# One decoder layer on one core: w_out gated earlier, four schedules around the MLP rewritten

## The chip, the cores and the metric

The kernel runs on one core of a Trainium2 chip. The metric is the device time of one execution in microseconds (us). TensorE (PE) does matmuls into PSUM, VectorE (DVE) and ScalarE (ACT) do the elementwise work, GpSimd (POOL) a little of it, and nearly all DMAs are issued from the queue of SyncE (SP). Each engine takes its instructions in a fixed order; an instruction that waits holds up all behind it on its engine.

## The reference

One layer (DEPTH 1) on x of 1024 tokens by 1024 features, fp32. Cut to what matters here:

```python
merged = sigmoid(ga) * (ya @ w_a) + sigmoid(gm) * (ym @ w_m)
x = x + gt_a * (merged @ w_out)                      # gt_a: one gate per output feature
h = rms_norm(x, norm_ffn_g) * (1 + sc_f) + sh_f
x = x + gt_f * (square(relu(h @ w_ff1)) @ w_ff2)     # 4096 hidden features
```

`ya` comes from an 8-head differential attention, `ym` from an mLSTM; both are computed before the part that changes, save the last attention head.

## The kernel before, in words

Every fp32 operand of a matmul is split into a high part (a rounded copy, written by ACT) and a low part (the difference, written by DVE; `parts`, lines 317 to 320), and a product is three matmuls. One call of `mm_block` is 12 matmuls of 128x512.

The large products are done by Strassen-Winograd: 7 block products in place of 8, numbered 1 to 7, with sums of blocks of the left operand, sums of blocks of the right operand, and sums of the outputs. These sums are DVE work. The stages, in order of time:

- **Last attention head beside w_m.** `at_core` (line 1202) for head 7 is woven with `m_unit` (line 1324): 32 half-steps of 12 matmuls for `ym @ w_m`, each output multiplied by its gate (`gated`, line 1312) and stored to `mb_d` from POOL's queue. 24 of the 32 are woven with the head, 8 come after it.
- **w_a, then w_out**, as two jobs of `Chunks` (line 1535). A chunk is 7 products of 48 matmuls (4 output rows of blocks, 12 each). `prep` makes the operands of a product one product ahead of `run`. `pieces` (line 1655) loads w_out in 8 pieces of 512 KB during the w_a job, and `behind` (line 1694) multiplies each piece by half the gate `gta` on DVE. `out_o` adds the residual rows `xr`, squares and sums them (`square`, `rms`), stores x to `xn_d` and scales the rows.
- **w_ff1** in 16 groups of 256 hidden features (`Ff1`, line 1820). `norm_feat` (line 1804) transposes the normalised rows and applies scale and shift, half on ACT and half on DVE. Groups 0 and 1 start while the right operands of products 7, 5, 6, 3 and 4 are still being made; each later group runs its 7 products of 12 matmuls. `out` applies relu and square; the blocks a11, a12, a21, a22 of the activation and their sums (7: a11-a21, 5: a21+a22, 6: that minus a11, 3: a12 minus that) are made on DVE and stored to `act_d[1..7]`, the left operands of the next stage.
- **w_ff2** as four chunks (lines 1998 to 2052). Chunk c needs the groups 4c to 4c+3. `fetch_act` loads a left operand (2 x 512 KB), `fetch_ff2` loads a block of w_ff2 and multiplies it by half the other gate on DVE. `out_f` adds each product to the accumulators `au, aa, av, ab, ac`, four of which are first loaded whole, 1 MB each, with the residual from `xn_d`.

The order of the instructions on each engine is not the program's: a planner simulates the program with its own costs, and issues whatever is ready and has a free buffer, earlier program text first. Buffers are drawn by tag (`BUFS`, line 57): "u" and "b" have 2 of 4 KB each, "e" and "v" 4, "r" 8, "f" 5 of 2 KB, "x" 4 large ones, "wh"/"wl" 2 each for split weights. A later tile of a tag waits until an earlier one has had its last reader. PSUM has three tags of 2, 3 and 3 banks; `Chunks.run` takes its four banks from one set or the other in turn (`self.sets`).

## Time and profile before

| what | value |
|---|---|
| median of 3 runs (lowest to highest) | 2050.91 us (2049.52 to 2053.59) |
| profiled execution: time, span | 2053.98 us, 2052.2 us |
| mean granted TensorE clock | 0.983 |
| PE busy | 1981.0 us, 97% |
| DVE busy | 1644.7 us, 80% |
| ACT busy | 1046.2 us, 51% |
| DMA | 296.71 MB, mean 145 GB/s |

The time is that of the profiled execution; the span runs from the first to the last instruction of its trace. Busy times overlap, and are averages over stages that have different limits: how near an engine is to its limit has to be read stage by stage. The granted clock is the share of full TensorE speed that the throttle allowed; where it is under 1, the same matmuls take longer while PE counts as busy.

### The profile page before, as it was taken

To read this page: it belongs to the slowest core of one execution; us is meant where nothing else is said; L and a number is where in the kernel's file an instruction comes from. 1 tells how busy PE (TensorE), PEld (TensorE's weight loads), DVE (VectorE), ACT (ScalarE), POOL (GpSimd) and SP (SyncE) were. 2 spreads that over 40 slices of the span, in tenths; PEclk is the share of its full clock that TensorE was granted. 3 is DMA by queue.
4 is the path that set the end of the run, shared out by engine and by line. 5 is a ranking of instruction groups with operands and counts; after the bars stand their busy time and mean duration, and the time that the engine had idled before them with its cause. 6 is when DMAs were issued, how large, how long until landed. Compare 5 with 4: busy or idle time off the path is not lost.

```text
span 2052.2 us, 30148 instructions
## 1 busy us (share of the span) xinstructions
PE 1981.0 (97%) x11193; PEld 1716.0 (84%) x11193; DVE 1644.7 (80%) x2892; ACT 1046.2 (51%) x1966; POOL 56.4 (3%) x150
## 2 busy tenths in 40 slices
PE   5999999999999999999999999999899999999999
PEld 5999988888888899999998788777688887788887
DVE  7977668987766568999979667999867767998896
ACT  5523324544656557777757535446544544433332
POOL 0000000000111000000000110000000000000000
PEclk7999999999999999999999999999999999999999
DMA  8376633336555342222223474513444447744531
GB/s 289 105 218 213 190 116 110 110 108 201 176 154 175 112 111 63 83 63 83 68 78 118 158 248 159 169 42 134 164 148 156 146 147 247 276 148 150 164 111 74
DMA packets 201834, 296.71 MB, mean 145 GB/s; under 512 B 13956, under 2 KB 114975, under 8 KB 201687
## 3 DMA queue, kind: packets, MB, share of 16 engines
q1 hardware_dynamic: 198806, 285.35, 43.4%
q0 software_dynamic: 2880, 9.44, 1.2%
q8 instruction: 88, 1.44, 0.3%
q14 instruction: 60, 0.48, 0.1%
HBM read 206.43 MB, written 79.93 MB: 140 GB/s over the span
## 4 chain that ended last, share of the span: by engine, by line
PE 74%; DVE 10%; DMA 7%; issue 4%; ACT 3%; POOL 1%; SPq 0%; POOLq 0%; DVEq 0%; ACTq 0%
PE cps L328 16%; PE pc L328 9%; PE pb L328 9%; PE pa L328 9%; PE pd L328 5%; PE ps L166 4%; PE ps L165 4%; PE ps L167 4%; PE lg L1219 3%; PE pv L1272 3%; DMA ex<-ea_d 2%; PE tp L1252 1%; PE ops L585 1%; DVE s_op L138 1%; DVE t_op L138 1%
## 5 line engine op out<-in xcount | busy, mean ns | idle before, releaser
L328 PE MATMUL cps<-t_op,s_op 128*128 128x512 f32 x2016 | 471.7, 395 | 11.7 <-ACT s_op L320 5.9
L328 PEld LDWEIGHTS cps<-t_op,s_op 128*128 128x128 f32 x2016 | 379.4, 189 | 101.2 <-ACT s_op L320 7.4
L320 ACT ACTIVATE w_op<-w_st 128x512 fp32r<-128x512 f32 (+1 forms) x197 | 135.8, 704 | 199.4 <-PE pb L328 61.7
L138 DVE TENSOR_TENSOR w_op<-w_st,w_op 128x512 fp32r<-128x512 f32 (+1 forms) x197 | 150.4, 782 | 25.1 <-ACT w_op L320 23.1
L165 PE MATMUL ps<-w_hi,hT 128*128 128x256 f32 x512 | 146.5, 286 | 0.0
L166 PE MATMUL ps<-w_lo,hT 128*128 128x256 f32 x512 | 145.9, 285 | 0.0
L167 PE MATMUL ps<-w_hi,hT 128*128 128x256 f32 x512 | 145.6, 284 | 0.0
L320 ACT ACTIVATE s_op<-act 128x1024 fp32r<-128x1024 f32 x56 | 58.5, 1051 | 144.7 <-PE cps L328 108.4
L1229 ACT ACTIVATE ee<-ee,mneg 128x256 f32<-128x256 f32 (+7 forms) x128 | 98.3, 769 | 10.0 <-DVE mneg L1225 9.7
L328 PE MATMUL pc<-bt,w_op 128*128 128x512 f32 x384 | 97.0, 399 | 6.1 <-ACT w_op L320 5.1
L1219 PE MATMUL lg<-kb,qe 128*128 128x512 f32 (+3 forms) x384 | 96.8, 360 | 5.0 <-DVE mneg L1225 4.4
L166 PEld LDWEIGHTS ps<-w_lo,hT 128*128 128x128 f32 x512 | 97.6, 191 | 1.4 <-issue 0.9
L165 PEld LDWEIGHTS ps<-w_hi,hT 128*128 128x128 f32 x512 | 97.5, 190 | 0.5
L167 PEld LDWEIGHTS ps<-w_hi,hT 128*128 128x128 f32 x512 | 97.6, 191 | 0.3
L328 PE MATMUL pa<-b,w_op 128*128 128x512 f32 x384 | 94.9, 397 | 0.4 <-DVE w_op L138 0.4
L328 PEld LDWEIGHTS pc<-bt,w_op 128*128 128x128 f32 x384 | 71.8, 190 | 26.5 <-ACT w_op L320 5.9
L316 DVE TENSOR_TENSOR acc<-cps,acc 128x512 f32<-128x512 f32 x116 | 77.0, 684 | 13.1 <-PE cps L328 12.8
L328 PEld LDWEIGHTS pa<-b,w_op 128*128 128x128 f32 x384 | 73.2, 192 | 15.9 <-DVE w_op L138 0.8
L1225 DVE CUSTOM_DVE_ANT_0 ee<-lg,bs 128x512 f32<-128x512 f32 (+4 forms) x128 | 69.9, 559 | 8.8 <-PE lg L1219 7.8
L138 DVE TENSOR_TENSOR s_op<-act,s_op 128x1024 fp32r<-128x1024 f32 x56 | 68.2, 1220 | 6.9 <-ACT s_op L320 6.9
L1219 PEld LDWEIGHTS lg<-kb,qe 128*128 128x128 f32 x384 | 61.2, 192 | 13.1 <-DVE mneg L1225 8.2
L328 PE MATMUL pa<-hT,w_op 128*128 128x512 f32 x264 | 64.1, 392 | 0.0
(404 smaller groups left out, 4747.8 us busy)
## 6 DMA issues: line engine op xcount, KB each, us to landing
w_st<-in_w_in_dram SPq DMA_DIRECT2D x72, 512.0 KB, 4.0
act<-act_d SPq DMA_DIRECT2D x56, 512.0 KB, 3.6
w_st<-in_w_ff_dram SPq DMA_DIRECT2D x36, 512.0 KB, 4.8
crow<-in_w_ada_dram SPq DMA_DIRECT2D x32, 512.0 KB, 4.3
w<-in_w_ff_dram SPq DMA_DIRECT2D x32, 512.0 KB, 4.8
act_d<-s SPq DMA_DIRECT2D x48, 256.0 KB, 2.0
wa<-in_w_ada_dram SPq DMA_DIRECT2D x16, 512.0 KB, 4.7
mq_d<-cv SPq DMA_DIRECT2D x16, 512.0 KB, 2.6
```

The source lines that it names most:

```text
L138: return (nc.gpsimd if pool else nc.vector).tensor_tensor(dst, src, hi.bitcast(F32), op=ALU.subtract)
L165: nc.tensor.matmul(o, lhsT=ah, rhs=bh, start=first, stop=False)
L166: nc.tensor.matmul(o, lhsT=ah, rhs=bl, start=False, stop=False)
L167: nc.tensor.matmul(o, lhsT=al, rhs=bh, start=False, stop=last)
L316: (nc.gpsimd if pick(pool, n) else nc.vector).tensor_tensor(o, a, b, op=ALU.add)
L320: nc.scalar.activation(dst[0], src, AF.Copy)
L328: nc.tensor.matmul(ps, lhsT=p, rhs=q, start=first and k == 0 and r == 0, stop=k == 3 and r == 2, skip_group_check=True,)
L585: nc.tensor.matmul(o, lhsT=a[ra], rhs=w[rb][:, k, :], start=k == 0 and ra == rb and j % 2 == 0, stop=k == KT - 1 and ra == 1, skip_group_c ...
L1219: nc.tensor.matmul(lg[:, 0:max(256, w)], lhsT=hd["q"][hf][e][:, r, q4 * P:(q4 + 1) * P], rhs=hd["k"][e][:, c0:c0 + max(256, w)], start=r = ...
L1225: nc.vector.tensor_tensor_reduce(ee[:, c0:c0 + w], lg[:, 0:w], hd["bs"][:, n - c0 - w:n - c0][:, ::-1], -0.125, first, ALU.add, ALU.min, last,
L1229: nc.scalar.activation(ee[:, 0:n], ee[:, 0:n], AF.Exp, bias=mneg[:, e:e + 1], scale=-1.0, accum_out=ssum[:, e:e + 1])
L1272: nc.tensor.matmul(pv[:, 0:256], lhsT=pts[kk // 4][r][:, (kk % 4) * P:(kk % 4 + 1) * P], rhs=v, start=kk == 0 and r == 0, stop=kk == qi an ...
```

## The change

It has five parts.

1. **w_out.** In the last attention head's stage, half the gate is made (`gta`), and 8 row blocks of w_out (128x1024, 512 KB) are loaded into "u" tiles, multiplied by it on DVE and stored to a new DRAM tensor `wo_d`, each load placed in the text with half-step 12, 14, ... 26 of `m_unit` and each multiplication and store three half-steps later. `pieces` then loads from `wo_d`, and `behind` is gone.
2. **First groups of w_ff1.** Groups 0 and 1 store their four blocks only; their four sums are made during groups 6 and 8 from blocks loaded back (`late_sums`). For groups 0 to 3 the square of the first block moves from DVE to ACT, and the second half of `norm_feat` is all on ACT.
3. **Last group of w_ff1.** A class of its own, with the product order 1, 6, 5, 3, 7, 4, 2; its four sums are made after the ninth product of w_ff2.
4. **First chunk of w_ff2.** Order 1, 2, 7, 4, 5, 6, 3, the bank sets begin with the other set, and the first values of `aa` and `av` are copied by ACT, as that of `au` was.
5. **Residual.** `ac` and `ab` are loaded whole after products 0 and 2; the residual of `aa` and `av` comes in 8 loads of 128x512, each added on DVE, around products 7 to 15.

```diff
--- before.py
+++ after.py
@@ -76,6 +76,7 @@
     xn_d = dp.tile([S, D], F32, name="xn_d")
     gt_d = dp.tile([2, P, D], F32, name="gt_d")
     ub_d = dp.tile([AH, S + P], F32, name="ub_d")
+    wo_d = dp.tile([D, D], F32, name="wo_d")
     ea_d = dp.tile([32, S], F32, name="ea_d")
 
 
@@ -1525,6 +1526,24 @@
         else:
             ym = ActX("ym")
             units = sum((m_unit(ym, u) for u in range(4)), [])
+            gta = wt("b", [P, D], "gta")
+            nc.sync.dma_start(gta, gt_d[0])
+
+            nc.vector.tensor_scalar(gta, gta, 0.5, None, op0=ALU.mult)
+            wos = {}
+
+            def fetch_wo(r):
+                wos[r] = wt("u", [P, D], "wor")
+                nc.sync.dma_start(wos[r], w_out[0][r * P:(r + 1) * P, :])
+
+            def gate_wo(r):
+                w = wos.pop(r)
+                nc.vector.tensor_tensor(w, w, gta, op=ALU.mult)
+                nc.sync.dma_start(wo_d[r * P:(r + 1) * P, :], w)
+
+            for r in range(8):
+                units[12 + 2 * r] = lambda r=r, f=units[12 + 2 * r]: (fetch_wo(r), f())
+                units[15 + 2 * r] = lambda r=r, f=units[15 + 2 * r]: (gate_wo(r), f())
             filler += reload(ym, ym_d, False) + units[0:12 * 2]
         weave(core, filler)
         late = nlate
@@ -1686,15 +1705,6 @@
     (m11, m21), (m12, m22), (u1, u2) = ((t[:, 0], t[:, 1]) for t in mgs)
     load[:] = [0.0, 0.0]
     ch = Chunks(xp.tile([P, 2, 4, 512], F32R, name="s_op", tag="x"))
-    gta = wp.tile([P, D], F32, name="gta", tag="ws", bufs=2)
-    nc.sync.dma_start(gta, gt_d[0])
-
-    nc.vector.tensor_scalar(gta, gta, 0.5, None, op0=ALU.mult)
-
-    def behind(t, c):
-        g = gta[:, c * 512:c * 512 + 512]
-        nc.vector.tensor_tensor(t, t, g.unsqueeze(1).to_broadcast([P, 2, 512]), op=ALU.mult)
-
     def merge(dst, c, f0, t0):
 
         mb = wt("m", [P, 512], "mb")
@@ -1731,13 +1741,13 @@
     for n in range(7):
         ch.prep()
         if n == 4:
-            wo = pieces("e", "wo", w_out[0], False, (11,), behind)
+            wo = pieces("e", "wo", wo_d, False, (11,))
         ch.run()
         if n == 5:
 
-            pieces("v", "wo", w_out[0], False, (21,), behind, wo)
-            pieces("e", "wo", w_out[0], False, (12,), behind, wo)
-            pieces("v", "wo", w_out[0], False, (22,), behind, wo)
+            pieces("v", "wo", wo_d, False, (21,), into=wo)
+            pieces("e", "wo", wo_d, False, (12,), into=wo)
+            pieces("v", "wo", wo_d, False, (22,), into=wo)
             xr = fetch("r", "xr", x2, range(8))
             ssq = cp.tile([P, NT, 2], F32, name="ssq")
             ssf = cp.tile([P, NT], F32, name="ssf")
@@ -1801,6 +1811,8 @@
 
     act_d = {i: dp.tile([NG * P, 512], F32, name=f"act{i}_d") for i in range(1, 8)}
 
+    ORDER_L = (1, 6, 5, 3, 7, 4, 2)
+
     def norm_feat(js, act, dst):
 
 
@@ -1837,7 +1849,10 @@
             c = into
             if c is None:
                 c = wt("f", [P, 512], "c")
-            if b is None:
+            if b is None and self.g < 4:
+                nc.scalar.activation(c, a, AF.Relu)
+                nc.scalar.activation(c, c, AF.Square)
+            elif b is None:
                 nc.scalar.activation(c, a, AF.Relu)
                 nc.vector.tensor_tensor(c, a, c, op=ALU.mult)
             else:
@@ -1850,10 +1865,13 @@
             elif (t, hf) == (1, 1):
                 self.a22 = c
                 self.put(4, c)
-                if self.g < 4:
+                if 1 < self.g < 4:
 
                     self.a11 = wt("f", [P, 512], "a11")
                     nc.sync.dma_start(self.a11, act_d[1][self.g * P:(self.g + 1) * P, :])
+            elif self.g in LATE:
+
+                self.put(5 if (t, hf) == (0, 1) else 2, c)
             elif (t, hf) == (0, 1):
 
                 s3 = wt("f", [P, 512], "s3")
@@ -1869,6 +1887,103 @@
                 sub(self.s24[:, 1], c, self.s24[:, 0], False)
                 self.put(3, self.s24[:, 1])
 
+    class Ff1Last(Ff1):
+
+
+        def weights(self, order):
+            (a11, a21), (a12, a22) = self.st
+            for q, i in enumerate(order):
+                if q % 2 == 0:
+                    t2 = w_tile().rearrange("p (s r k c) -> p s r k c", s=2, r=2, k=4)
+                src = {1: a11, 2: a12, 4: a22, 5: a21, 6: a11, 7: a11, 3: None}[i]
+                if i == 6:
+                    add(a21, a21, a22, *self.pool)
+                    sub(a11, a21, a11, *self.pool)
+                elif i == 3:
+                    src = self.s3()
+                    sub(src, a12, a11, *self.pool)
+                elif i == 7:
+
+                    sub(a11, a22, a11, *self.pool)
+                self.operand(i, t2[:, q % 2], src)
+
+        def p6(self):
+            pd, m1 = bank("mm", "pd"), self.m1[0]
+            self.prod(6, 0, pd, True)
+            add(m1, pd, m1, False)
+
+        def p5(self):
+            self.pb[0] = bank("pa", "pb5")
+            self.m7[0] = wt("m", [P, 512], "m7")
+            self.prod(5, 0, self.pb[0], True)
+            nc.scalar.activation(self.m7[0], self.pb[0], AF.Copy)
+
+        def p7(self):
+            m7 = self.m7[0]
+            self.pc[0] = bank("pb", "pc")
+            self.prod(7, 0, self.pc[0], True)
+            add(m7, self.pc[0], m7, False)
+            self.out(1, 1, 0, m7, self.m1[0], m7)
+
+        def out(self, t, hf, n, a, b, into):
+            c = into
+            if c is None:
+                c = wt("f", [P, 512], "c")
+            if b is None:
+                nc.scalar.activation(c, a, AF.Relu)
+            else:
+                add(c, a, b, False)
+                nc.scalar.activation(c, c, AF.Relu)
+            nc.scalar.activation(c, c, AF.Square)
+            if (t, hf) == (0, 1):
+                self.a21 = c
+            elif (t, hf) == (1, 1):
+                self.a22 = c
+                self.put(4, c)
+            elif (t, hf) == (1, 0):
+                self.a12 = c
+                self.put(2, c)
+            else:
+                self.put(1, c)
+                self.a11 = c
+
+        def sums(self):
+            a11, a12, a21, a22 = self.a11, self.a12, self.a21, self.a22
+            s3 = wt("f", [P, 512], "s3")
+            sub(s3, a11, a21, False)
+            self.put(7, s3)
+            add(a21, a21, a22, False)
+            self.put(5, a21)
+            sub(a11, a21, a11, False)
+            self.put(6, a11)
+            sub(a12, a12, a11, False)
+            self.put(3, a12)
+
+    LATE = (0, 1)
+
+    def late_sums(g):
+
+        x, y = (wt("e", [P, 2, 512], "late") for _ in range(2))
+        a11, a21, a22, a12 = x[:, 0], x[:, 1], y[:, 0], y[:, 1]
+
+        def fetch():
+            for v, i in ((a11, 1), (a21, 5), (a22, 4), (a12, 2)):
+                nc.sync.dma_start(v, act_d[i][g.g * P:(g.g + 1) * P, :])
+
+        def one():
+            add(a22, a21, a22, False)
+            g.put(5, a22)
+            sub(a21, a11, a21, False)
+            g.put(7, a21)
+
+        def two():
+            sub(a11, a22, a11, False)
+            g.put(6, a11)
+            sub(a12, a12, a11, False)
+            g.put(3, a12)
+
+        return fetch, one, two
+
 
     eb = [wt("e", [P, 2, 512], f"eb{k}") for k in range(4)]
     e_at = lambda k: eb[k // 2][:, k % 2, :]
@@ -1882,7 +1997,7 @@
             B[i] = lambda k: (ts[k][:, 0, :], ts[k][:, 1, :])
 
     feat0 = norm_feat(range(4), (4, 5, 6, 7), e_at)
-    groups = [Ff1(g) for g in range(NG)]
+    groups = [Ff1(g) for g in range(NG - 1)] + [Ff1Last(NG - 1)]
     g0, g1, g2, g3 = groups[0:4]
 
     def half0(k):
@@ -1901,7 +2016,7 @@
     g1.load_first()
     rw = [wt("r", [P, 2, 512], "rw") for _ in range(4)]
     b_at = lambda k: rw[k // 2][:, k % 2, :]
-    feat1 = norm_feat(range(4, 8), (4, 5, 6, 7), b_at)
+    feat1 = norm_feat(range(4, 8), range(8), b_at)
 
     def right(i, k):
         b11, b21, b12, b22 = e_at(k), e_at(4 + k), b_at(k), b_at(4 + k)
@@ -1987,19 +2102,23 @@
         if g in (g2, g3):
             g.weights((7, 5, 6, 3, 4))
             run([g.p7, g.p5, g.p6, g.p3, g.p4])
+        elif g.g in (6, 8):
+            fetch, one, two = late_sums(groups[LATE[g.g // 2 - 3]])
+            g.weights((1, 7, 2, 5, 6, 3, 4))
+            run([fetch, g.p1, g.p7, g.p2, g.p5, one, g.p6, two, g.p3, g.p4])
         elif g is not groups[-1]:
             g.weights((1, 7, 2, 5, 6, 3, 4))
             run([g.p1, g.p7, g.p2, g.p5, g.p6, g.p3, g.p4])
         else:
-            g.weights((1, 7, 2, 5, 6, 3, 4))
-            run([g.p1, g.p7, g.p2, g.p5, g.p6, g.p3, g.p4])
+            g.weights(ORDER_L)
+            run([getattr(g, f"p{i}") for i in ORDER_L])
 
 
     def out_f(c, i, j, ps):
         d = {1: au, 7: av, 2: aa, 4: ac, 5: av, 6: au, 3: ab}[i]
         last = c == NC - 1
-        if i == 1 and c == 0:
-            nc.scalar.activation(au[:, j], ps, AF.Copy)
+        if c == 0 and i in (1, 2, 7):
+            nc.scalar.activation(d[:, j], ps, AF.Copy)
         elif i != 6 or not last:
             add(d[:, j], ps, d[:, j], False)
         if last:
@@ -2029,27 +2148,44 @@
         ms = {2: (11,), 3: (12,), 4: (22,), 5: (21,)}.get(n, ())
         fetch_ff2(c + 1, w2[c + 1], [(m, homes[c + 1][m]) for m in ms])
 
+    ORDER_F = [(1, 2, 7, 4, 5, 6, 3) if not c else ORDER_X for c in range(NC)]
     for c in range(NC):
         ch.add(
-            ORDER_X, None, w2[c], lambda i, j, ps, c=c: out_f(c, i, j, ps),
+            ORDER_F[c], None, w2[c], lambda i, j, ps, c=c: out_f(c, i, j, ps),
             lambda i, q, c=c: act.pop((c, i, q)),
         )
-    order = [(c, i) for c in range(NC) for i in ORDER_X]
+    order = [(c, i) for c in range(NC) for i in ORDER_F[c]]
+    ch.sets = 1
     fetch_act(0, 1)
     ch.prep()
+    fetch_ff2(0, w2[0], [(21, homes[0][21])])
+    fetch_act(0, 2)
     fetch_ff2(0, w2[0], [(12, homes[0][12]), (22, homes[0][22])])
     fetch_act(0, 7)
-    for q, t0, c0 in ((aa, 0, 0), (ab, 0, 512), (ac, 512, 0), (av, 512, 512)):
-        nc.sync.dma_start(q, xn_d[t0:t0 + 512, c0:c0 + 512].rearrange("(t p) c -> p t c", p=P))
-    fetch_ff2(0, w2[0], [(21, homes[0][21])])
-    fetch_act(0, 2)
     fetch_act(0, 4)
+
+    whole = {0: (ac, 512, 0), 2: (ab, 0, 512)}
+    joins = [(q, t0, c0, j) for q, t0, c0 in ((aa, 0, 0), (av, 4, 512)) for j in range(4)]
+    rows = {}
+
     for n in range(7 * NC):
         if n + 4 < len(order):
             fetch_act(*order[n + 4])
         ch.prep()
         chunk_part(n // 7, n % 7)
         ch.run()
+        if n == 8:
+            groups[-1].sums()
+        if n in whole:
+            q, t0, c0 = whole[n]
+            nc.sync.dma_start(q, xn_d[t0:t0 + 512, c0:c0 + 512].rearrange("(t p) c -> p t c", p=P))
+        if n - 1 in rows:
+            q, t0, c0, j = joins[n - 8]
+            add(q[:, j], q[:, j], rows.pop(n - 1), False)
+        if 7 <= n < 15:
+            q, t0, c0, j = joins[n - 7]
+            rows[n] = wt("m", [P, 512], "res")
+            nc.sync.dma_start(rows[n], xn_d[(t0 + j) * P:(t0 + j + 1) * P, c0:c0 + 512])
 
 
 # ---- launch: one core; inputs and outputs as the reference has them ----
```

## The prediction

> **What bounds the kernel now.** I read the page's busy times first, then the stretches of 50 us, then the waits of PE in the stretches where it idles.
>
> ```profile
> PE 1981.0 (97%) x11193; PEld 1716.0 (84%) x11193; DVE 1644.7 (80%) x2892; ACT 1046.2 (51%) x1966; POOL 56.4 (3%) x150
> ```
>
> The change adds and removes no matmul, so what it can win is idle time of PE (2052.2 - 1981.0 = 71 us of the span) and time at a lower granted clock. Here are the stretches it touches; columns are busy us of PE, PEld, DVE, ACT, POOL with instruction counts, then granted clock, DMA share, GB/s.
>
> ```profile
> 1100.00:1150.00 50.00, 42.67 (x223) 35.30 (x223) 45.15 (x118) 37.90 (x90) 2.66 (x4) 0.90 0.51 159
> 1150.00:1200.00 50.00, 49.88 (x250) 41.82 (x249) 29.03 (x49) 17.41 (x35) 4.39 (x8) 1.00 0.56 190
> 1300.00:1350.00 50.00, 45.20 (x186) 35.26 (x185) 50.00 (x67) 22.24 (x30) 0.00 (x0) 0.97 0.25 84
> 1400.00:1450.00 50.00, 46.20 (x205) 36.84 (x205) 46.22 (x78) 31.34 (x57) 1.77 (x2) 0.93 0.40 130
> 1450.00:1500.00 50.00, 43.93 (x182) 34.55 (x181) 38.07 (x62) 24.75 (x42) 0.00 (x0) 0.97 0.55 186
> 1550.00:1600.00 50.00, 50.00 (x218) 40.47 (x217) 34.89 (x56) 26.08 (x43) 0.00 (x0) 1.00 0.42 145
> 1700.00:1750.00 50.00, 45.76 (x191) 36.23 (x190) 37.56 (x50) 23.90 (x36) 0.00 (x0) 0.97 0.78 272
> 1750.00:1800.00 50.00, 47.63 (x207) 38.24 (x206) 46.80 (x49) 19.64 (x20) 0.00 (x0) 1.00 0.72 251
> 1815.00:1893.00 78.00, 78.00 (x341) 63.77 (x340) 71.32 (x80) 28.51 (x32) 0.00 (x0) 1.00 0.46 144
> ```
>
> PE is full wherever it is not starved. It is starved in four places, and the waits of PE there (us in total, times, longest) say by whom: 1300 to 1360 (w_out begins), 1360 to 1430 and 1430 to 1500 (w_ff1 begins), 1720 to 1800 (w_ff2 begins).
>
> ```profile
> PE cps L328 <- ACT t_op L320: 2.7, 1, 2.7
> PE cps L328 <- DVE t_op L138: 2.3, 3, 1.6
> ...
> PE tp L1810 <- DVE xr L1761: 2.0, 1, 2.0
> ...
> PE pc L328 <- ACT w_op L320: 5.1, 2, 3.7
> PE pd L328 <- ACT w_op L320: 1.0, 1, 1.0
> PE pc L328 <- DVE w_op L138: 1.0, 1, 1.0
> PE pd L328 <- DVE w_op L138: 0.4, 1, 0.4
> ...
> PE cps L328 <- ACT s_op L320: 5.9, 3, 3.2
> PE cps L328 <- DVE s_op L138: 0.7, 1, 0.7
> ```
>
> So 5.0, 2.0, 7.5 and 6.6 us. Each longer gap is followed by a stretch at a lower clock:
>
> ```profile
> 1340.00:1350.00 10.00, 6.78 (x22) 4.78 (x22) 10.00 (x15) 6.13 (x10) 0.00 (x0) 0.83 0.00 1
> 1400.00:1410.00 10.00, 7.65 (x27) 5.42 (x27) 9.02 (x17) 4.83 (x11) 1.77 (x2) 0.72 0.45 159
> 1460.00:1470.00 10.00, 6.30 (x21) 4.27 (x20) 9.78 (x17) 5.53 (x10) 0.00 (x0) 0.83 0.96 348
> 1740.00:1750.00 10.00, 6.81 (x24) 5.13 (x23) 8.95 (x12) 5.59 (x8) 0.00 (x0) 0.83 1.01 369
> ```
>
> A clock of 0.83 over 10 us costs 1.7 us, one of 0.72 costs 2.8. I charge 1.7 to each of the first, third and fourth place.
>
> **1. The gating leaves the w_out stage.** The tile view of `wo`: eight multiplications, and the DVE idle time before them, which waits on the loads.
>
> ```profile
> L1696 DVE TENSOR_TENSOR wo<-wo,gta x8: 1216/1224/1229, 1264.3 to 1310.1; 128x1024 f32<-128x1024 f32 x8
> ...
> DMA wo<-in_w_out_dram: 7.4, 4
> ...
> 1308.93 2.36 DVE L1696 TENSOR_TENSOR wo<-wo,gta 128x1024 f32<-128x1024 f32 x2
> ```
>
> DVE loses 8 x 1.22 = 9.8 us of work and up to 7.4 us of waiting, all ahead of 1311. From 1300 to 1350 it is busy for all 50 us, so a backlog is what starves PE, and 5.0 us of PE waiting need less relief than that. The last two multiplications, 2.36 us, stand directly before the operands of the first w_out product. Eight loads of the same size remain, now from `wo_d`. Value -(5.0 + 1.7) = -6.7; bounds -6.7 and 0 (the DVE finds other waits). I take -6.7, since 17.2 us of relief against 5.0 leaves a wide margin.
>
> **2. The gating arrives beside w_m.** Added on DVE: 8 x 1.22, and the scaling of `gta`, which it only moves by some tens of us: 9.8 us. Between 1150 and 1200 DVE is busy 29 of 50 us, so 21 us are free in that stretch alone while PE is full: nothing, as long as the stretch is PE's; without that cover 9.8 us. Added on SP: 8 loads, 8 stores and the earlier `gta` load, 8.5 MB in all. The stretch at risk is the one ahead of it, 1120 to 1150:
>
> ```profile
> 1120.00:1130.00 10.00, 6.58 (x30) 4.05 (x28) 9.74 (x36) 8.37 (x27) 0.54 (x1) 1.00 0.95 284
> ...
> 1121.31 6.40 SPq L1663 DMA_DIRECT2D wa<-in_w_a_dram  x4
> ...
> 1138.20 1.06 ACT L152 ACTIVATE w_hi<-w_st 128x1024 fp32r<-128x1024 f32 x1 [1.47 <-DMA w_st<-in_w_m_dram]
> ```
>
> The planner there puts four loads of w_a, wanted 100 us later, ahead of w_m's; ACT then waits for w_m with the softmax of the head behind it. The "u" and "b" buffers fall free at about that time, so the first two w_out loads and `gta` (1.5 MB) can go the same way: at 284 GB/s that is 5.5 us of DMA. Bounds 0 (they are issued after w_m's) and +5.5; no work leaves this stretch, which excludes a gain. I take +2, between the ends, because only a part of a shared delay falls on w_m's loads.
>
> **3. First groups of w_ff1.** Columns: min/median/max ns.
>
> ```profile
> L1815 DVE TENSOR_SCALAR rw<-tp,gsf,shf x4: 804/805/811, 1411.0 to 1424.2; 128x512 f32<-128x512 f32 x4
> ...
> L1842 DVE TENSOR_TENSOR c<-pa,c x16: 684/692/693, 1417.3 to 1720.2; 128x512 f32<-128x512 f32 x16
> ...
> L1813 ACT ACTIVATE rw<-tp,shf,gsf x4: 767/773/776, 1414.0 to 1425.1; 128x512 f32<-128x512 f32 x4
> ...
> 1463.46 0.68 DVE L313 TENSOR_TENSOR s<-c,a 128x512 f32<-128x512 f32 x1
> 1464.06 0.68 DVE L313 TENSOR_TENSOR s<-w_st 128x512 f32<-128x512 f32 x1
> ```
>
> DVE loses 8 sums (8 x 0.68), 4 squares (4 x 0.69) and 4 scalings (4 x 0.81): 11.4 us between 1411 and 1466. The sums stand right before the line `s<-w_st` at 1464.06, from which ACT makes the weight that ended PE's longest wait, 3.7 us. ACT gains 4 x 0.77 and 4 squarings of about the same length, some 6 us, in a stretch where it is busy 31 of 50 us. Of the 7.5 us of waits, 2.4 (the second `pc` wait of 5.1 - 3.7 = 1.4, and the 1.0 for DVE) come where group 3 starts behind group 2's sums, and these stay. So -(7.5 - 2.4 + 1.7) = -6.8; bounds -6.8 and 0 (ACT becomes what is late). I take -6, near the full end, as DVE had no idle time there. The moved sums go to groups 6 and 8 (1550 to 1650), where DVE has 15 of 50 us free: 8 x 0.68 and 8 loads of 256 KB, hidden by it; 5.4 us if not. The wait of 2.0 us at 1404 has its DVE chain before the scalings moved, so I leave it: 0, bounds -(2.0 + 2.8) and +2.
>
> **4. Start of w_ff2.** PE waits there for ACT, and ACT for a transfer:
>
> ```profile
> 1744.71 1.06 ACT L320 ACTIVATE s_op<-act 128x1024 fp32r<-128x1024 f32 x1 [1.17 <-DMA act<-act_d]
> ...
> L2043 SPq DMA_DIRECT2D acc<-xn_d x4: 386/481/590, 1715.8 to 1739.3; - x4
> ...
> DMA to landing us min/median/max: 10.0/10.0/10.0
> ```
>
> The DMA share is 1.01 from 1740 to 1750, and 4 MB of the queue are the residual: at that row's 369 GB/s they are 11 us, and the third product's wait is 5.9 + 0.7 in all. Afterwards the first three products need 2, 2 and 3 MB instead of 2, 3 and 2, with no residual ahead of them; at 369 GB/s a product of 11 us covers 4 MB. The four sums of the last group (4 x 0.68 on DVE) and their four stores go as well. -(6.6 + 1.7) = -8.3 at best, 0 if the new order of the last group frees its buffers too late. I take -6.5, as DVE, too, is nearly full there (46.8 of 50).
>
> **5. Chunks 0 and 1 of w_ff2.** Chunk 0 moves 8 adds to ACT copies; chunk 1 gets 8 residual adds and the 4 sums: 12 x 0.68 = 8.2 us. In 1815 to 1893, about one chunk, DVE is busy 71.3 of 78 us: 6.7 free, 1.5 short. Bounds 0 and +8.2 (cover gone); I take +1.5.
>
> **Sum.** -6.7 + 2 - 6 - 6.5 + 1.5 = -15.7 us. The profiled execution took 2053.98 us, 3 above the median of the runs; -15.7 on the median of 2050.91 is 2035.
>
> [...]
>
> **The rivals.**
> - *Slower: the round trip of w_out jams the queues beside w_m.* Only two "u" buffers serve eight load-multiply-store turns, so each load waits on SP until the store two turns before has landed, and the w_m, gate and w_a loads stand behind it. The tile that holds the split left operand of w_a's first products is drawn from the same "u" and "b" buffers, so w_a cannot prepare before the last turn is over. For it: the loads of w_a at 1121 show that the planner lets such work pass. Against: the stretch has 90 us and PE runs full in it. It decides when a turn's store (2.6 us for 512 KB, row below) is no longer covered by w_m work in hand: 8 x 2.6 = 20.8, and a clock loss of 1.7; -15.7 - 2 + 22.5 = +4.8, so 2056.
>
> ```profile
> mq_d<-cv SPq DMA_DIRECT2D x16, 512.0 KB, 2.6
> ```
>
>   [...]
> - *Half: the w_out stage stays as it is* because DVE's backlog there is made of splits and merges (1300 to 1350 has 65 other instructions), and w_ff2's start wins half: -15.7 + 6.7 + 3 = -6, so 2045. For it: DVE is full for 50 us. Against: the 17 us of relief.
> - *No change: the waits are renamed.* A planner that orders anew gives back elsewhere what it wins; 2051. For it: DVE is above 90% in most of the stages concerned.
>
> **How the numbers follow.** Likeliest 2035 with 0.64; half 0.14; no change 0.09; slower 0.13. The likeliest one's own range is 2026 to 2043: all terms at their good ends give -6.7 - 6.8 - 8.3 - 4.8 = -26.6, 2024, which is unlikely together. The range of 8 in 10 goes from 2024 to 2050. A measurement here can tell about 0.2%, 4.1 us: faster (under 2046.8) 0.64 + 0.11 = 0.75; same 0.03 + 0.09 = 0.12; slower 0.13.
>
> **What would show it.** Right: from w_out's first product on no PE wait over 1 us for `t_op`; no wait of 3 us on `w_op` as w_ff1 begins; no wait of ACT on `act` as w_ff2 begins, with the granted clock at 1.00 around it; PE still full in the chunk after the first. Step 2 is wrong if PE's idle time between 1120 and 1150 grows by over 5 us. The whole is wrong if the four places keep over half of their 21 us, or if PE starts w_a late.

## The result and the profile after

The changed kernel takes 2039.85 us (median of 6 runs, 2033.00 to 2041.01); the kernel before, run beside it, 2053.06 us (6 runs, 2049.52 to 2059.35). The ratio is 0.9927, 95% interval 0.9912 to 0.9943: faster, by 13.2 us in the medians. The profiled execution after is one of the short ones, 2033.65 us with a span of 2031.9; the profiled pair is 20.3 us apart, and 4.6 of that lies ahead of all that was changed.

To see this I cut both traces at five places. First the timeline of before, then that of after: the start of the last head (ACT), the first product of w_a (PE), the first transpose of w_ff1 (PE), the first product of w_ff2 (PE) and the last sum of the output (DVE). Columns: start us, us, engine, line, operation.

```profile
1096.67 1.04 ACT L1168 ACTIVATE sq<-raw 128x1024 f32<-128x1024 f32 x1
1233.86 26.44 PE L328 MATMUL cps<-t_op,s_op 128*128 128x512 f32 x114
1392.20 0.66 PE L1810 MATMUL tp<-ksq,xr 128*128 128x128 f32 x4 [0.32 <-DVE xr L316]
1730.21 2.10 PE L328 MATMUL cps<-t_op,s_op 128*128 128x512 f32 x8 [0.32 <-ACT s_op L320]
2048.45 0.69 DVE L316 TENSOR_TENSOR acc<-cps,acc 128x512 f32<-128x512 f32 x1 [2.03 <-PE cps L328]
```

```profile
1092.08 1.04 ACT L1169 ACTIVATE sq<-raw 128x1024 f32<-128x1024 f32 x1
1236.06 24.10 PE L329 MATMUL cps<-t_op,s_op 128*128 128x512 f32 x104
1388.50 0.66 PE L1822 MATMUL tp<-ksq,xr 128*128 128x128 f32 x4 [0.31 <-DVE xr L317]
1718.11 22.24 PE L329 MATMUL cps<-t_op,s_op 128*128 128x512 f32 x96
2028.01 0.69 DVE L317 TENSOR_TENSOR acc<-cps,acc 128x512 f32<-128x512 f32 x1 [2.03 <-PE cps L329]
```

The differences are four stages: **A** last head and w_m, **B** w_a and w_out, **C** w_ff1, **D** w_ff2. The same cuts were made in every kernel below (us):

| kernel | A | B | C | D |
|---|---|---|---|---|
| before | 137.2 | 158.3 | 338.0 | 318.2 |
| after | 144.0 | 152.4 | 329.6 | 309.9 |
| only_w_out | 142.4 | 154.7 | 340.0 | 317.0 |
| no_w_out | 134.3 | 158.8 | 328.6 | 309.7 |
| only_first | 135.4 | 158.6 | 329.4 | 317.9 |
| only_ff2 | 137.0 | 159.8 | 337.8 | 309.5 |
| dma_only | 143.4 | 152.5 | 328.8 | 310.6 |
| dve_only | 137.4 | 154.0 | 330.3 | 310.1 |
| pool_wm | 151.5 | 154.4 | 329.7 | 310.9 |
| no_w_out_pool | 137.6 | 161.3 | 329.9 | 309.7 |
| late_gates | 134.4 | 163.9 | 329.6 | 309.7 |
| sums_only | 143.6 | 155.7 | 334.3 | 310.7 |
| res_whole | 145.9 | 154.1 | 328.8 | 310.7 |
| last_plain | 143.4 | 155.4 | 331.2 | 312.4 |

What comes ahead of stage A is the same work in all of them, yet it took from 1091 to 1100 us. A stage is therefore a better measure of one part than a total is. Here are the stretches of after that answer to those shown of before; columns as there.

```profile
1150.00:1200.00 50.00, 44.86 (x227) 37.35 (x226) 30.68 (x50) 17.55 (x35) 3.83 (x7) 1.00 0.82 283
1200.00:1250.00 50.00, 47.17 (x216) 38.71 (x215) 31.71 (x41) 19.09 (x30) 5.40 (x9) 1.00 0.52 177
1300.00:1350.00 50.00, 48.23 (x208) 38.63 (x207) 48.94 (x66) 25.26 (x37) 0.00 (x0) 1.00 0.22 72
1400.00:1450.00 50.00, 49.34 (x226) 40.64 (x227) 46.15 (x78) 36.34 (x66) 1.07 (x1) 0.97 0.39 114
1450.00:1500.00 50.00, 47.63 (x201) 38.27 (x200) 33.07 (x53) 25.00 (x42) 0.00 (x0) 0.97 0.56 188
1700.00:1750.00 50.00, 50.00 (x219) 40.49 (x218) 44.50 (x49) 29.76 (x44) 0.00 (x0) 1.00 0.94 333
1750.00:1800.00 50.00, 50.00 (x219) 40.88 (x218) 46.07 (x52) 20.20 (x23) 0.00 (x0) 1.00 0.57 187
1800.00:1900.00 100.00, 100.00 (x437) 81.66 (x436) 93.88 (x110) 35.34 (x38) 0.00 (x0) 1.00 0.54 168
```

At w_out's start PE is busy 48.2 of 50 us, before 45.2. As w_ff1 begins it is 49.3 and 47.6, before 46.2 and 43.9. As w_ff2 begins it is full. The loss is in the first two rows: 44.9 and 47.2, where before had 49.9 and 50.0. The waits of PE in after, in two stretches (1100 to 1240, then 1245 to 1500), name what is left:

```profile
PE pv L1273 <- DVE ptl L1257: 4.0, 3, 3.1
...
PE tp L1290 <- DVE yt L1284: 2.2, 1, 2.2
PE ps L166 <- DVE sg L1320: 1.7, 1, 1.7
...
PE tp L1822 <- DVE xr L1771: 2.0, 1, 2.0
PE cps L329 <- DVE t_op L139: 1.8, 1, 1.8
PE pc L329 <- ACT w_op L321: 1.4, 1, 1.4
PE pc L329 <- DVE w_op L139: 1.0, 1, 1.0
```

The first three do not stand in before's list for the same stretch, whose waits of PE come to 7.4 us against 15.0 here. Summing each stage over windows of 2 us puts the changes in the same places: PE's idle time goes from 7.5 to 15.1 us in A, from 5.4 to 2.1 in B, from 10.2 to 4.7 in C and from 6.3 to 0.3 in D. The clock loss, the sum of 2 us times (1 - granted clock), goes from 5.1, 1.7, 5.1 and 1.7 us to 1.7, 0, 3.4 and 0. Idle time and clock loss together change by +4.2, -5.0, -7.2 and -7.7 us, where the stages of these two traces change by +6.8, -5.9, -8.4 and -8.3. So 2.6 us of A, and about 1 us of each other stage, stay unexplained.

### The profile page after: what moved, and what is told of

It is laid out like the page before. It is cut to its first block, busy times and chain, and to the rows that moved or that the text cites. A ratio compares the mean times of both kernels' runs of the same rounds, so it can differ in the third digit from the quotient of the medians.

```text
span 2031.9 us, 30206 instructions
## 1 busy us (share of the span) xinstructions
PE 1970.7 (97%) x11193; PEld 1709.9 (84%) x11193; DVE 1636.7 (81%) x2883; ACT 1053.0 (52%) x1983; POOL 55.8 (3%) x150
## 4 chain that ended last, share of the span: by engine, by line
PE 77%; DVE 8%; DMA 6%; issue 4%; ACT 4%; POOL 1%; SPq 0%; DVEq 0%; POOLq 0%; ACTq 0%
PE cps L329 18%; PE pa L329 10%; PE pc L329 10%; PE pb L329 10%; PE pd L329 5%; PE ps L167 4%; PE ps L166 4%; PE ps L168 4%; PE lg L1220 3%; PE pv L1273 2%; DMA ex<-ea_d 1%; PE ops L586 1%; PE tp L1253 1%; DMA w<-in_w_ff_dram 1%; DMA xt<-in_x_dram 1%
## 5 line engine op out<-in xcount | busy, mean ns | idle before, releaser
L329 PE MATMUL cps<-t_op,s_op 128*128 128x512 f32 x2016 | 466.8, 393 | 2.1 <-DVE t_op L139 1.8
L167 PE MATMUL ps<-w_lo,hT 128*128 128x256 f32 x512 | 145.9, 285 | 0.0
L317 DVE TENSOR_TENSOR acc<-cps,acc 128x512 f32<-128x512 f32 x108 | 71.5, 682 | 11.0 <-PE cps L329 11.0
L139 DVE TENSOR_TENSOR s_op<-act,s_op 128x1024 fp32r<-128x1024 f32 x56 | 68.2, 1218 | 6.6 <-ACT s_op L321 6.5
```

What stands on the lines that cost most here:

```text
L139: return (nc.gpsimd if pool else nc.vector).tensor_tensor(dst, src, hi.bitcast(F32), op=ALU.subtract)
L167: nc.tensor.matmul(o, lhsT=ah, rhs=bl, start=False, stop=False)
L317: (nc.gpsimd if pick(pool, n) else nc.vector).tensor_tensor(o, a, b, op=ALU.add)
L329: nc.tensor.matmul(ps, lhsT=p, rhs=q, start=first and k == 0 and r == 0, stop=k == 3 and r == 2, skip_group_check=True,)
```

## The experiments

**Which part does what.** Part 1 (w_out), part 2 (first groups) and parts 3 to 5 together (last group, first chunk, residual) were each put alone into the kernel before, and part 1 was taken out of the changed kernel.

```diff
 only_w_out: before + part 1        no_w_out: after - part 1
 only_first: before + part 2        only_ff2: before + parts 3, 4, 5
```

> The kernel before with part 1 alone: w_out gated beside w_m, the rest as before. Stage lengths are read from the profile between four landmarks: start of the last head's norm, first w_a product, first transpose of w_ff1, first w_ff2 product, last add. Before they are 137.2, 158.3, 338.0 and 318.2 us; in the changed kernel 144.0, 152.4, 329.6 and 309.9. Theory A (each part acts in its own stage, and the round trip of w_out costs as much as it wins): first stage near 144, second near 152, the other two as before; total within 3 us of before. Theory B (the prediction: the round trip costs 2 us): first stage near 139, total about 4.7 us under before.

> The changed kernel with part 1 undone: w_out gated in its own stage on VectorE, as before; parts 2 to 5 kept. Theory A: first two stages as before (137 and 158 us), the other two as changed (330 and 310), total as the changed kernel within 3 us, some 13 us under before. Theory B: total 4.7 us above the changed kernel.

> The kernel before with part 2 alone: the late sums of groups 0 and 1, the squares and the scalings on ScalarE. Theory A: only the third stage changes, by -8 us (338 to 330), no PE wait of 3 us on w_op as w_ff1 begins; total -8. Theory C (ScalarE becomes what is late, and the gain of this stage needs the other parts): under half of it, -4 or less.

> The kernel before with parts 3, 4 and 5 alone: last group, first chunk, residual. Theory A: the third stage as before, the fourth 310 instead of 318 us with no wait of ScalarE on act as w_ff2 begins; total -8. Theory C (the start of w_ff2 is won because the earlier sums are already gone): the fourth stage keeps over half of its waits, -4 or less.

| kernel | median us | ratio to before, 95% interval |
|---|---|---|
| only_w_out | 2056.41 | 1.0013 (1.0000 to 1.0027) |
| no_w_out | 2035.58 | 0.9920 (0.9895 to 0.9946) |
| only_first | 2046.01 | 0.9969 (0.9954 to 0.9985) |
| only_ff2 | 2044.72 | 0.9964 (0.9951 to 0.9978) |

Part 1 wins nothing: alone it is at best as fast as before, and without it the changed kernel is not slower. By the stage table it takes 4.4 us from B (mean 154.5 with it in after, only_w_out, sums_only, res_whole and last_plain; 158.9 without it in before, no_w_out, only_first and only_ff2) and adds 7.9 to A (143.9 against 136.0). Part 2 takes 9.4 from C (329.2 in after, no_w_out and only_first; 338.6 in before, only_w_out and only_ff2). Parts 3 to 5 take 8.0 from D (309.7 in after, no_w_out and only_ff2; 317.7 in the other three). The sum is -4.4 + 7.9 - 9.4 - 8.0 = -13.9, against -13.2 in the medians, so the parts add up.

**What part 1 costs beside w_m: the traffic or DVE's work.** Both of these leave the gate out of the result. The first keeps all loads and stores and drops the eight multiplications. The second keeps the eight multiplications on two loaded tiles, drops the other six loads and the stores, and loads w_out itself later.

```diff
 dma_only
-                nc.vector.tensor_tensor(w, w, gta, op=ALU.mult)
 dve_only
-                wos[r] = wt("u", [P, D], "wor")        # each r
+                if r < 2: ...                          # load two only
-                nc.sync.dma_start(wo_d[r * P:(r + 1) * P, :], w)
-            wo = pieces("e", "wo", wo_d, False, (11,))
+            wo = pieces("e", "wo", w_out[0], False, (11,))
```

> The changed kernel without the multiplication beside w_m: the eight loads and stores of w_out stay, so that wo_d holds w_out without its gate (the gate is left out of the result). Without the round trip the first stage took 134 to 137 us, with it 142 and 144. Theory D (the traffic delays the stores of the w_m outputs, and with them VectorE's buffers and the softmax): first stage stays at 142 to 144. Theory E (VectorE stands before a multiplication whose load has not landed): first stage back at 134 to 138.

> The changed kernel with the eight multiplications beside w_m but only two of the eight loads and no store; the w_out stage loads w_out itself, so the gate is left out of the result. Theory D: first stage back at 134 to 138. Theory E: it stays at 142 to 144, or in between if VectorE's 9.8 us of work is what costs.

Stage A: 143.4 us with the traffic alone, 137.4 with the multiplications alone (totals 2034.57 and 2028.87, one run each). The 8 MB of loads and stores cost it, and DVE's 9.8 us are hidden, as the prediction had it. That holds for the stage as a whole; the way from the traffic to PE is not the same in every kernel. From 1120 to 1210 the DMAs moved 18.58 MB before and 25.21 MB after. The DMA views of that stretch, before and then after, show one store that suffers; columns are count, KB each, median us to landing.

```profile
DMA packets 11094, 18.58 MB, mean 206 GB/s; under 512 B 773, under 2 KB 4869, under 8 KB 11088
...
mb_d<-sg POOLq DMA_DIRECT2D x11, 256.0 KB, 2.6
```

```profile
DMA packets 13650, 25.21 MB, mean 280 GB/s; under 512 B 961, under 2 KB 6081, under 8 KB 13644
...
mb_d<-sg POOLq DMA_DIRECT2D x10, 256.0 KB, 5.3
```

The store of w_m's gated output lands after 5.3 us where it took 2.6. Its "f" buffer is what the softmax's `ptl` of the last head waits for. In after's timeline of DVE:

```profile
1172.73 0.42 DVE L1257 TENSOR_TENSOR ptl<-tp,pth 128x256 fp32r<-128x256 f32 x1 [4.73 <-DMA mb_d<-sg]
...
1204.66 0.69 DVE L1257 TENSOR_TENSOR ptl<-tp,pth 128x512 fp32r<-128x512 f32 x1 [2.63 <-DMA mb_d<-sg]
```

These two waits (7.4 us, before 1.8) stand ahead of PE's waits of 4.0 us for `ptl`. The other traces bear this link out. In the five kernels that have part 1 and compute the whole layer with its multiplications on DVE, the store lands after 4.9 to 5.5 us, DVE waits 5.5 to 7.4 us for it ahead of `ptl`, and PE 1.3 to 4.4 us for `ptl`. In the seven without the stores to `wo_d` (before, no_w_out, only_first, only_ff2, dve_only, late_gates, no_w_out_pool) these are 2.3 to 3.0, 0.7 to 2.2 and 0 to 0.7 us.

In dma_only the store is as late (5.2 us), but PE waits only 0.7 us for `ptl`. There the traffic reaches PE by another way: ACT waits 7.2 us for a store to `wo_d` before it may write the split left operand of w_a, which takes a "u" buffer of the round trip. The softmax's `pth` stands right behind it on ACT, and PE behind that. From dma_only's timelines of ACT and PE:

```profile
1174.70 1.06 ACT L321 ACTIVATE s_op<-wa 128x1024 fp32r<-128x1024 f32 x1 [7.16 <-DMA wo_d<-wor]
1175.66 0.85 ACT L1256 ACTIVATE pth<-tp 128x512 fp32r<-128x512 f32 x2
...
1176.29 1.65 PE L1273 MATMUL pv<-va,pth 128*128 128x256 f32 x6 [3.84 <-ACT pth L1256]
```

In the five kernels named above this wait of ACT is 0.3 us. So shown is that the transfers cost it, and that the late store of `mb_d` is a link of it wherever the whole of part 1 is there. The link is only a part of the 7.9 us: the other waits of A are not followed up here. Nor is it shown how much comes from the load on the DMAs and how much from the order in SP's queue, where in after the stores to `wo_d` wait 20.3 us for their multiplications (1120 to 1240). ACT's wait for the gate loads, which SP issues too, did not grow from before to after (23.6 and 23.4 us from 1100 to 1240).

**GpSimd in place of DVE.** The multiplications went to GpSimd, once beside w_m (pool_wm) and once in their old place in stage B (no_w_out_pool, part 1 undone).

```diff
 pool_wm
-                nc.vector.tensor_tensor(w, w, gta, op=ALU.mult)
+                nc.gpsimd.tensor_tensor(w, w, gta, op=ALU.mult)
 no_w_out_pool, in behind()
-        nc.vector.tensor_tensor(t, t, g..., op=ALU.mult)
+        nc.gpsimd.tensor_tensor(t, t, g..., op=ALU.mult)
```

> The changed kernel with the eight multiplications beside w_m on GpSimd. Theory D: first stage still 142 us or more, since the traffic is the same and the stores of the w_m outputs are issued from GpSimd's queue, behind the multiplications. Theory E: first stage 134 to 138.

> Parts 2 to 5 kept, part 1 undone, and the gating of w_out in its own stage put on GpSimd, with no round trip through DRAM. If what starves TensorE in that stage is VectorE's work and its waits on the loads: first stage 136, second 153 instead of 159, total some 5 us under the kernel with part 1 undone (0.9895 of before). If a multiplication on GpSimd is so slow (no row shows one of that size) that the first pieces are late, or if it slows VectorE: second stage 159 or more, no gain.

Stage A became 151.5 us in pool_wm, the longest of all (2050.69 us, one run); what made it longer than the traffic alone did is open. In no_w_out_pool stage B became 161.3 instead of 158.8; it took 2040.62 us, ratio 0.9921 (0.9900 to 0.9943). DVE had been given 9.8 us of room and did not keep it. DVE's groups from 1260 to 1312 (busy us, mean ns; idle before), in no_w_out and then in no_w_out_pool:

```profile
L1696 DVE TENSOR_TENSOR wo<-wo,gta 128x1024 f32<-128x1024 f32 x8 | 9.7, 1224 | 7.8 <-DMA wo<-in_w_out_dram 7.8
...
L138 DVE TENSOR_TENSOR t_op<-yar,t_op 128x1024 fp32r<-128x1024 f32 x6 | 7.3, 1218 | 0.0
...
L316 DVE TENSOR_TENSOR mg<-sg,mb 128x512 f32<-128x512 f32 x8 | 5.3, 684 | 0.0
```

```profile
L138 DVE TENSOR_TENSOR t_op<-yar,t_op 128x1024 fp32r<-128x1024 f32 x7 | 12.3, 1759 | 0.0
...
L138 DVE TENSOR_TENSOR s_op<-wa,s_op 128x1024 fp32r<-128x1024 f32 x7 | 8.5, 1216 | 5.7 <-ACT s_op L320 5.7
L316 DVE TENSOR_TENSOR mg<-sg,mb 128x512 f32<-128x512 f32 x6 | 8.2, 1376 | 0.0
L316 DVE TENSOR_TENSOR mg<-cps,mg 128x512 f32<-128x512 f32 x12 | 7.9, 678 | 1.9 <-PE cps L328 1.9
```

Operations of DVE that fell beside the GpSimd multiplications grew: `t_op` from 1218 to 1759 ns on average, `mg<-sg,mb` from 684 to 1376. Those that read a PSUM tile (`mg<-cps,mg`, 678) did not, nor did `s_op<-wa,s_op` (1216), which reads SBUF twice. The timelines of DVE and GpSimd (POOL) in no_w_out_pool show when; here they are merged by start:

```profile
1267.33 1.23 DVE L138 TENSOR_TENSOR s_op<-wa,s_op 128x1024 fp32r<-128x1024 f32 x1 [1.57 <-ACT s_op L320]
1267.69 3.13 POOL L1696 TENSOR_TENSOR wo<-wo,gta 128x1024 f32<-128x1024 f32 x1 [1.44 <-DMA wo<-in_w_out_dram]
...
1269.07 2.83 DVE L138 TENSOR_TENSOR t_op<-yar,t_op 128x1024 fp32r<-128x1024 f32 x1
```

Whichever began first kept its length (GpSimd's 2.42 at 1279.39 and 2.40 at 1286.72, DVE's 1.23 and 1.21). Beside the six multiplications up to 1294, the four DVE operations with two SBUF inputs that began while one ran took 2.83, 3.43, 2.66 and 2.90 us in place of 1.21 or 0.68, and ended 0.5 to 1.1 us after it. Where DVE's operation had begun 0.4 and 0.1 us before (`s_op` here, `wo<-wo` at 1290.19), GpSimd's took 3.13 and 3.40 us in place of 2.40. The rows show when the second one took longer, and not what made it.

**A version without the round trip.** In no_w_out DVE waits 7.8 us for the w_out loads (first row of its list above), ahead of the operands that PE then misses. late_gates lets the same eight multiplications come later in DVE's order, pinned among the merges.

```diff
-            wo = pieces("e", "wo", w_out[0], False, (11,), behind)
+            wo = pieces("e", "wo", w_out[0], False, (11,))
+        if n == 5: gate(11)        # 21 after that product, 12 with the next, 22 in the w_out job
```

> The changed kernel with part 1 undone, and the eight gating multiplications, which stand ahead of w_out's first operands, set later in DVE's order among the merges of w_a's last groups, so that each comes when its load has landed. Theory G (what starves PE at w_out's first product is the 7.8 us that DVE waits on those loads, not the 9.8 us of multiplying): from the first w_a product to the first w_ff1 transpose 153 to 155 us (158.8 with the gates early, 152.4 in the changed kernel), nothing added beside w_m (134 to 138 us), total about 2031, ratio 0.989 to 0.991. Theory H (the multiplications themselves are too much for DVE there, wherever they stand): that stretch stays at 158 us or longer, total about 2036, ratio 0.992.

B became 163.9 us, longer than 158.8; 2039.59 us in all, ratio 0.9932 (0.9910 to 0.9954). The waits on loads are gone, and two waits stand in their place, DVE's from 1250 to 1330 and PE's from 1225 to 1370:

```profile
DVE s_op L138 <- ACT s_op L320: 8.0, 3, 5.4
...
PE cps L328 <- DVE t_op L138: 6.3, 2, 4.6
```

DVE idled 8.0 us for ACT in place of the 7.8 for the loads, and then had the multiplications still to do (the last at 1320.7) when PE wanted its operands. Moving the waits did not empty DVE's full stretch. This order falls; whether another one would do better is open. No kernel tried that computes the whole layer is shown faster than the changed one: no_w_out's interval overlaps with it.

**Part 2 split.** sums_only keeps the late sums, and gives the squarings and the four scalings back to DVE.

```diff
-            if b is None and self.g < 4:
-                nc.scalar.activation(c, a, AF.Relu)
-                nc.scalar.activation(c, c, AF.Square)
-            elif b is None:
+            if b is None:
-    feat1 = norm_feat(range(4, 8), range(8), b_at)
+    feat1 = norm_feat(range(4, 8), (4, 5, 6, 7), b_at)
```

> The changed kernel with the late sums of the first two groups of w_ff1, but its squarings and its four scalings back on DVE. Before, w_ff1's stretch (first w_ff1 transpose to first w_ff2 product) took 338.0 us, in the changed kernel 329.6. Theory L (the late sums give nearly all, since they stood right before the operand of PE's longest wait): 330 to 332. Theory M (DVE's whole backlog counts, and 6.0 of its 11.4 us are scalings and squarings): 333 to 335.

C: 334.3 us, 4.3 of the 9.4 us (2044.39 in all, one run). The waits of PE in C that after does not have, or has shorter (the first is 1.0 there):

```profile
PE pc L329 <- DVE w_op L139: 1.5, 2, 1.0
...
PE pb L329 <- ACT w_op L321: 1.1, 1, 1.1
PE pd L329 <- ACT w_op L321: 1.0, 1, 1.0
```

The wait of 3.7 us is gone, and waits of 1 us remain. Removing the sums ahead of that one weight was not enough; the 6 us of squarings and scalings are worth about as much (5.1 us of the stage) as the 5.4 us of sums. By this one run, the whole backlog of DVE counts.

**Parts 3 to 5 split.** res_whole loads the residual whole again, behind the operands of products 1, 2 and 7. last_plain has the last group's old order and sums, and the old order of the PSUM sets.

```diff
 res_whole
-        if c == 0 and i in (1, 2, 7):
+        if c == 0 and i == 1:
+    for q, t0, c0 in ((aa, 0, 0), (ab, 0, 512), (ac, 512, 0), (av, 512, 512)):
+        nc.sync.dma_start(q, xn_d[...])                # after fetch_act(0, 7)
-        (the loads in whole, rows and their adds)
 last_plain
-    ORDER_L = (1, 6, 5, 3, 7, 4, 2)
+    ORDER_L = (1, 7, 2, 5, 6, 3, 4)
-    groups = [Ff1(g) for g in range(NG - 1)] + [Ff1Last(NG - 1)]
+    groups = [Ff1(g) for g in range(NG)]
-    ch.sets = 1
-        if n == 8: groups[-1].sums()
```

> The changed kernel with the residual loaded whole, 4 MB at the start of w_ff2 as before, and with the new order of the last group and of chunk 0 kept. From the first w_ff2 product to the last sum of the output: 317.7 us before, 309.9 in the changed kernel. Theory R (the residual's 4 MB held back the operands' loads): 313 to 318, with an ACT wait on the transfer of act of over 1 us. Theory O (the order of the products did it, and the DMA queue has room for the residual once operands come in the new order): 310 to 312.

> The changed kernel with the last group of w_ff1 in its old order and its sums at once, as the other groups have them, and with chunk 0's order and the residual's late loads kept. From the first w_ff2 product to the last sum of the output: 317.7 us before, 309.9 in the changed kernel. Theory R (the residual alone did it): 310 to 311. Theory O (the last group's results must be there early): 313 or more, with waits of PE on operands of chunk 0.

With the residual whole, D is 310.7 us and C and D together 639.5, the same as in after (639.5). With the old last group D is 312.4, and C and D together 643.6, half of the way back to only_first (647.3), which has none of parts 3 to 5; D alone lies between the two expectations. One run each (2040.81 and 2047.24). ACT's wait on `act` as D begins, 1715 to 1800, and PE's there, in res_whole:

```profile
ACT s_op L321 <- DMA act<-act_d: 2.4, 2, 2.2
...
PE cps L329 <- ACT s_op L321: 1.1, 1, 1.1
```

ACT's wait of 2.2 us for a transfer ended before D began, and PE waited 1.1 us in D, where before its waits for ACT there were 5.9. So the 4 MB may be loaded at once and cost nothing measurable, where the operands of the first three products stand ahead of them in the queue. Late loading, and part 5's adds and ACT copies with it, gave nothing measurable here either.

Were the operands in `act` what PE missed before? The trace of only_first, which keeps the old order and the old residual, says no. Its D is as long as before (317.9 us), and PE's three waits for ACT come to 5.5 us, yet ACT waits only 0.3 us for `act` from 1715 to 1800 (before: 1.5). The two long waits of PE lead to DVE, to the gate multiplications of the w_ff2 blocks (L1978), in before:

```profile
1738.62 1.23 DVE L1978 TENSOR_TENSOR w<-w,gtf 128x1024 f32<-128x1024 f32 x1 [2.75 <-DMA w<-in_w_ff_dram]
...
1757.66 2.19 ACT L320 ACTIVATE t_op<-w 128x1024 fp32r<-128x1024 f32 x2 [8.76 <-DVE w L1978]
```

Ahead of the second product DVE waits for a w_ff2 block (2.8 us, in only_first 3.7), so the right operand that ACT makes of it comes late, and the left operand stands behind that in ACT's order. In before 1.2 us of `act` come on top; in only_first none do, and PE still waits 2.8 us there, before 3.2. Ahead of the third, ACT waits 8.8 us for two multiplications, in both kernels, and they stand in DVE's order behind three sums of `acc` that wait for PE. In after DVE's wait for such a block is 0.2 us. Whether the residual held that block back is not shown.

The last group's order and late sums gave about 4 of the 8 us; the new order of the first chunk alone was not tried, so how the other 4 divide is open.

## Why the prediction was right or wrong

The time was right: 2035 predicted, 2039.85 measured, inside the likeliest case's own range of 2026 to 2043. The gain was -15.7 by the sum and -13.2 by the medians. But single terms were off by up to 5.9 us and cancelled, so that the sum came this near is luck in part.

- **1, gating leaves w_out:** -6.7 predicted, -4.4 measured. PE's waits went from 5.0 us to 1.8, and the clock loss from 1.7 to none; that no wait over 1 us would be left for `t_op` was wrong. "A wide margin" of relief was the failing step: DVE is still busy 48.9 of 50 us from 1300 to 1350, so the backlog is mostly its other work, as the rival "half" had it. late_gates points the same way.
- **2, gating arrives beside w_m:** +2 predicted, bounds 0 to +5.5, and +7.9 measured, outside the bounds. That DVE's 9.8 us are hidden was right (dve_only). The failing step was "the stretch at risk is the one ahead of it, 1120 to 1150": there PE's idle time did not grow (7.3 us before, 5.8 after). I costed only the first 1.5 MB, and took 1150 to 1200 as safe because PE was full there. In that stretch the DMA share was 0.56, and went to 0.82; stores that had landed in 2.6 us took 5.3. The prediction's sign for step 2 therefore looked in the wrong place, and its sign that the whole is wrong, "if PE starts w_a late", came true in this stage: PE starts w_a 6.8 us later after the head's start than before.
- **The slower rival** (the round trip jams the queues, 22.5 us) named the right cause and the wrong price, about a third of it real. The link in after is not the one that it named: the late store is in POOL's queue, and SP's waits for stores to `wo_d` are 4.4 us (1120 to 1240). Its second mechanism, w_a's left operand that waits for a buffer of the round trip, cost 0.3 us of ACT's time there; in dma_only it held ACT for 7.2 us and PE for 3.8.
- **3, first groups:** -6 predicted with -6.8 as the best end, and -9.4 measured. In the first 100 us of C the idle time fell from 9.9, 10.2 and 10.3 us (before, only_w_out, only_ff2) to 4.7, 4.9 and 5.1 (after, no_w_out, only_first): -5.2, the 5.1 of waits that the term held. The clock loss fell from a mean of 5.1 to 2.3, so 2.8 for the 1.7 charged; the last 1.4 has no place in the trace that I can name. The waits of 2.0, 1.4 and 1.0 stayed, as said. The reason was half right: sums_only shows that the sums before `s<-w_st` were not the whole cause.
- **4 and 5, w_ff2:** -6.5 + 1.5 = -5.0 predicted, -8.0 measured. The size of term 4 at its best end, -8.3, came true: PE's idle time in D went from 6.3 to 0.3 and the clock loss from 1.7 to none. Its mechanism did not, so this is luck. The step "PE waits there for ACT, and ACT for a transfer" failed: ACT's wait for `act` was 1.5 us before and 0.3 in only_first, where PE waited about as long; DVE's gate multiplications stood behind both long waits. The 6.6 us are also not the third product's alone: 1.1 fall on the first product, 3.2 on the second and 2.4 on the third. And the sign "no wait of ACT on `act`" did not come true: ACT waits 1.3 us for it in after while PE is full. That the 4 MB of the residual cost time, by way of a late w_ff2 block perhaps, is not shown; res_whole shows that they need not. Term 5 was 0 and not +1.5: in the 100 us from 1800 DVE is busy 93.9, and PE all 100.

The sum of what was wrong, +2.3 + 5.9 - 3.4 - 3.0, is +1.8 us: the range held for the total, and not for the terms.

## What to carry to other kernels

Before moving work to a place where an engine has room, price its transfers there too: here a stretch with PE full and the DMAs at half load (49.9 of 50 us, a share of 0.56) was part of a stage that lost 7.9 us to 8 MB of extra traffic, where the move won 4.4 elsewhere. Where an engine is full for 50 us, count its whole backlog, and not only the instructions just before the longest wait of another. A wait on a transfer is the cause of the engine's wait behind it only if the two go together: look for a run in which the first shrinks, as ACT's wait for `act` did in only_first, and see whether the second stays.

## What the runs showed of the hardware

**The half-speed clock came in lumps.** Summed by windows of 2 us, the clock loss was a multiple of 1.7 us in every stage of before and after, which at the granted clock of 0.50 in the second row of the stretches below is 3.4 us. In that row PE did 5 matmuls in 2 busy us, in the last one, at 1.00, 10. PE's timeline of before, and its stretches:

```profile
1745.82 12.66 PE L328 MATMUL cps<-t_op,s_op 128*128 128x512 f32 x48 [3.19 <-ACT s_op L320]
1760.85 9.45 PE L328 MATMUL cps<-t_op,s_op 128*128 128x512 f32 x39 [2.37 <-ACT s_op L320]
```

```profile
1744.00:1746.00 2.00, 0.18 (x1) 0.18 (x2) 2.00 (x4) 1.06 (x1) 0.00 (x0) 0.91 1.05 407
1746.00:1748.00 2.00, 2.00 (x5) 1.61 (x6) 2.00 (x3) 1.39 (x2) 0.00 (x0) 0.50 1.04 393
...
1760.00:1762.00 2.00, 1.15 (x5) 0.97 (x6) 2.00 (x3) 2.00 (x3) 0.00 (x0) 1.00 1.06 390
1762.00:1764.00 2.00, 2.00 (x10) 1.45 (x9) 2.00 (x3) 1.65 (x2) 0.00 (x0) 1.00 0.56 206
```

A gap of 3.19 us was followed by half speed (0.50), and so was one of 2.71 (w_out's start; 0.57 from 1346 to 1348); one of 2.37 was not (1.00 from 1760 to 1764). A gap of 1.99 us at 1402 was followed by 6.8 us of it (a loss of 3.4; 0.50 from 1406 to 1410), but behind that gap came 1.5 us of transposes and another gap of 0.36, and which of the two gaps it followed is not shown. So these gaps of 1.99 to 3.19 us cost themselves, or themselves and one or two lumps of 1.7, and nothing in these rows tells which it will be.

**GpSimd's multiplications were no free help to DVE.** One of 128x1024 took 2.4 to 3.4 us there and 1.22 on DVE, where `t_op` and `mg<-sg,mb`, with two SBUF inputs each, grew by 0.54 and 0.69 us on average beside them (no_w_out_pool against no_w_out). Up to 1294 the DVE operations with two SBUF inputs that began while one ran took 2.66 to 3.43 us; where DVE's had begun 0.4 and 0.1 us before, GpSimd's took 3.13 and 3.40.
